# A decoder block on one core: GpSimd's convolution sums issued in halves, and one pair's weight differences moved behind the feed-forward's last split

## The chip, the cores and the metric

The kernel runs on one core of a Trainium2 chip. The metric is device microseconds from launch to the last output. It is given as the median of several runs; one more run was recorded by the hardware profiler, and all durations below come from that one.

Five engines work side by side, each through its own queue in order: PE (TensorE, matrix products, with its weight loads PEld), DVE (VectorE), ACT (ScalarE), POOL (GpSimd), and SP, which here only issues transfers. Semaphores hold an instruction back until what it needs is there.

## What is computed

The input is x, 256 tokens of width 1024, and 256 memory tokens. The reference, cut to the steps that matter here:

```
h = rms_norm(x)
u_conv, q, kc, vc, ks, vs, kw, vw, g_nsa_heads, g_conv, g_attn = split(h @ w_in)
a, gt = split(u_conv)
v = a * sigmoid(gt)
v = depthwise_causal_conv(v, conv_dw_w, width 31) + conv_dw_b
conv = silu(layer_norm(v)) @ conv_pw_w
nsa = sparse attention with 16 heads (compressed, selected, windowed keys)
x = x + (sigmoid(g_conv) * conv + sigmoid(g_attn) * nsa) @ w_out
x = x + cross_attention(rms_norm(x), mem)
a, b = split(rms_norm(x) @ ffn_in_w)
x = x + (silu(a) * b) @ ffn_out_w            # 2816 hidden units
return rms_norm(x)
```

Everything is float32.

## The kernel before

**Products.** A float32 product is made on PE from parts: each operand is split into a high part, a rounded copy, and a low part, the rest. Three products (high by high, low by high, high by low) are summed. The split of an operand is always a copy on ACT (names ending in `h`, L174 in `split`, L283 in `part`) and a subtraction on DVE that reads the operand and the copy (names ending in `l`, L175 and L284). The weights come from HBM in tiles of 128 x 1024 elements, each loaded by SP, split so, and read by PE. So PE needs a stream of ACT copies and DVE subtractions through the whole kernel.

**The convolution.** The products for `u` fill `vt` (L449), 1024 channels as eight blocks of 128 partitions, two blocks to a tile. Each block is convolved with 31 taps. The blocks are shared out. DVE makes one part in PSUM (`taps_v`, accumulator `yp`, L402 and L405), one multiply-add of 128 x 256 per tap and block. GpSimd sums the other part (`taps_g`): for each tap and pair of blocks a product tile `vw` of 128 x 512 is made, two instructions of 128 x 256, on ACT (L419) or, for every sixth tap, on GpSimd itself (L417). GpSimd then adds it to `yt` (L421). There are four buffers for `vw`, so ACT can be at most four taps ahead of GpSimd's sums. `joined` (L425) adds DVE's part to GpSimd's for the blocks that both worked on. `layer_norm_sum` (L611, L613) sums the eight blocks of `yt` into `ysum` on GpSimd, `folded` adds its two halves (L292), and PE forms the mean from it (`mu`, L619). These operations lie beside the products for `u`, `kc`, `vc`, `q`, `ks`, `kw`, `vs`, `ga` and `gc`, so that ACT and DVE carry convolution work and weight splits in one queue each.

**The feed-forward.** For each of 22 chunks j PE makes `ps_f` (L1140, L1142), then ACT and DVE make `ab` (L1143 to L1145), `sl` (L1147, L1148) and its split `uh`, `ul` (L283, L284). `marks` are the two instructions of that split of the chunk made last; after the loop they are those of chunk 21.

**The output product.** It takes 11 pairs of chunks. Six of them (`SEVEN`: 1, 2, 4, 5, 7, 8) use seven products of half-size blocks in place of eight; these need differences of weight blocks, `tr`, four DVE subtractions of 128 x 512 per pair (`side`, L1084). For pair 1, `weights_ahead` makes them early, piece by piece. For the others `weights_of_seven` loads the weights (`fo`, L1090, into the four buffers named `w`), makes `tr`, and splits weights and differences: `th`, `tl` for every other pair, `ft` for the rest. `seven_products` issues the matrix products (L1172). The tail (L1207 to L1273) adds the parts, normalizes and stores.

**The order.** A scheduler orders each engine's instructions by priority and by the times that it reckons with. `convolve` puts its instructions 1500 places behind where they are written, so that they fill gaps. `behind(*marks)` forbids that what is written inside it be issued ahead of the marks.

Of the kernel before, what the change touches and what calls it, by code (L numbers as in the profile page):

```python
# [12 lines left out]
ALU = mybir.AluOpType  # L13
# [32 lines left out]
SEVEN = (1, 2, 4, 5, 7, 8)  # L46
# [51 lines left out]
def tile_hybrid_block(  # L98
# [15 lines left out]
    nc = tc.nc  # L114
# [6 lines left out]
    def long(name, slot, shape=(P, NB, S), dt=F32):  # L121

        return sb.tile(list(shape), dt, tag=f"L{slot}", name=name)
# [9 lines left out]
    def small(name, shape, dt=F32, tag=None, bufs=1):  # L133
        return sb.tile(shape, dt, tag=tag or name, name=name, bufs=bufs)
# [31 lines left out]
    def col(base, j):  # L166
        return ppt[:, base + j:base + j + 1]


    def split(w, shape, name):  # L170
        hi = small(f"{name}h", shape, F32R, tag="whi", bufs=5)
        lo = small(f"{name}l", shape, F32R, tag="wlo", bufs=5)
        with behind(*first.get(name, ())):
            copy = nc.scalar.activation(hi, w, AF.Copy)  # L174
            splits[name] = copy, nc.vector.tensor_tensor(out=lo, in0=w, in1=f(hi[:]), op=ALU.subtract)  # L175
        return hi, lo
# [4 lines left out]
    def behind(*marks):  # L181

        stack = ExitStack()
        for m in marks:
            stack.enter_context(tc.issue_after(m.ins))
        return stack
# [22 lines left out]
    def half(src, name):  # L209
        w = small(name, list(src.shape), tag="w", bufs=4)  # L210
        nc.sync.dma_start(w, src)
        return split(w, list(src.shape), name)
# [69 lines left out]
    def part(hi, lo, src):  # L282
        copy = nc.scalar.activation(hi, src, AF.Copy)  # L283
        low = nc.vector.tensor_tensor(out=lo, in0=src, in1=f(hi), op=ALU.subtract)  # L284
        return copy, low

    def folded(a, eng):

        n = a.shape[1]
        while n > 1:  # L290
            n //= 2
            eng.tensor_tensor(out=a[:, 0:n], in0=a[:, 0:n], in1=a[:, n:2 * n], op=ALU.add)  # L292
        return a[:, 0]
# [79 lines left out]
    for i in range(4):  # L373
        hs = slice(2 * i, 2 * i + 2)
        for kb in (2 * i, 2 * i + 1):
            vec = nc.vector.scalar_tensor_tensor(out=hf[:, kb], in0=xt_t[:, kb], scalar=col(PP_GMIX, kb),
                                                 in1=r1, op0=ALU.mult, op1=ALU.mult)
# [14 lines left out]
    yt = long("yt", 6)  # L392
# [16 lines left out]
    def taps_g(j, ts):  # L409

        y = yt[:, j:j + 2]
        for t in ts:
            pr = y if t == 0 else small(f"vw{j}_{t}", [P, 2, S], tag="vw", bufs=4)
            for i in range(2):
                v, w = vt[j + i][:, t:t + S], col(PP_DW + TAPS * (j + i), t)
                if t % MIX == MIX - 1:
                    nc.gpsimd.tensor_scalar(out=pr[:, i], in0=v, scalar1=w, scalar2=0.0, op0=ALU.mult, op1=ALU.add)  # L417
                else:
                    nc.scalar.activation(pr[:, i], v, AF.Identity, scale=w, bias=col(PP_DB, j + i) if t == 0 else 0.0)  # L419
            if t > 0:  # L420
                nc.gpsimd.tensor_tensor(out=y, in0=y, in1=pr, op=ALU.add)  # L421
            yield

    def joined(j, other):
        nc.gpsimd.tensor_tensor(out=yt[:, j:j + 2], in0=yt[:, j:j + 2], in1=other, op=ALU.add)  # L425
        yield


# [1 line left out]
    taps = range(TAPS)  # L430
    on_v = chain(taps_v(0, taps[FIRST_G:], part01), taps_v(2, taps, yt[:, 2:4]), taps_v(6, taps[LAST_G:], part67))
    on_g = chain(taps_g(0, taps[:FIRST_G]), joined(0, part01), taps_g(6, taps[:LAST_G]), taps_g(4, taps), joined(6, part67))

    def convolve(n_v, n_g, *marks):
# [172 lines left out]
    ysum = small("ysum", [P, 2, S], tag="vw", bufs=4)  # L607

    def layer_norm_sum():

        nc.gpsimd.tensor_tensor(out=ysum, in0=yt[:, 0:2], in1=yt[:, 2:4], op=ALU.add)  # L611
        for j in (6, 4):
            nc.gpsimd.tensor_tensor(out=ysum, in0=ysum, in1=yt[:, j:j + 2], op=ALU.add)  # L613
        return folded(ysum, nc.gpsimd)

    def layer_norm_centre(total):
# [208 lines left out]
    nc.vector.tensor_tensor(out=sumc, in0=sumc, in1=cpt[:, CP_CM:CP_CM + 2].unsqueeze(2).to_broadcast([P, 2, HEADS]), op=ALU.mult)  # L825
    vec = nc.vector.tensor_tensor(out=nsc, in0=nsc, in1=sumc.unsqueeze(3).to_broadcast([P, 2, HEADS, 16]), op=ALU.mult)
    total = layer_norm_sum()
    rest(10)
    pct = small("pct", [P, 2, S], tag="vw", bufs=4)
    for hp, n in enumerate((7, 7, 6, 6, 6, 6, 6, 4)):  # L830
        if hp < 7:
            with behind(*[vec] * (hp == 0)):
                p.append(scores(hp + 1))
            if hp == 0:
                first["gc1_0"] = first["scores"]
                with behind(*first["scores"]):
                    hm = cpt[:, CP_HM:CP_HM + 8].unsqueeze(2).to_broadcast([P, 8, HD])
                    for i in range(2):
                        nc.vector.tensor_tensor(out=vcm[:, 8 * i:8 * i + 8], in0=vcs[:, i].unsqueeze(1).to_broadcast([P, 8, HD]),
                                                in1=hm, op=ALU.mult)  # L840
# [239 lines left out]
    def side(tr, w, n):  # L1080

        to, a, b = SIDES[n]
        pick = lambda c: tr[:, c] if isinstance(c, int) else w[c[0]][:, c[1]]
        return nc.vector.tensor_tensor(out=tr[:, to], in0=pick(a), in1=pick(b), op=ALU.subtract)  # L1084

    def weights_of_seven(i):

        w0, w1 = w = [small(f"fo{i}_{n}", [P, 2, 512], tag="w", bufs=4) for n in range(2)]
        for n in range(2):
            nc.sync.dma_start(w[n], wfo[i, n])  # L1090
        tr = long(f"tr{i}", 10, (P, 4, 512))
        for n in range(4):
            side(tr, w, n)
        b0, b1 = split(w0[:, 0:1], [P, 1, 512], f"fo{i}_0"), split(w1, [P, 2, 512], f"fo{i}_1")
        bs = [[t[:, 0] for t in b0], [t[:, 0] for t in b1], [t[:, 1] for t in b1]]
        if SEVEN.index(i) % 2 == 0:
            th, tl = (long(f"t{c}{i}", at, (P, 4, 512), F32R) for c, at in (("h", 12), ("l", 13)))
            for n in (0, 2):
                part(th[:, n:n + 2], tl[:, n:n + 2], tr[:, n:n + 2])
            ts = [[t[:, n] for t in (th, tl)] for n in range(4)]  # L1100
        else:
            ts = []
            for n in (0, 2):
                both = split(tr[:, n:n + 2], [P, 2, 512], f"ft{i}_{n}")
                ts += [[t[:, k] for t in both] for k in range(2)]
        return bs + ts
# [25 lines left out]
    for j in range(NF):  # L1132
# [16 lines left out]
        marks = part(uh[j // 8][:, j % 8], ul[j // 8][:, j % 8], sl[:])  # L1149
# [67 lines left out]
    for i in range(early):  # L1217
        if i in SEVEN:
            if i not in parts:
                parts[i] = weights_of_seven(i)  # L1220
            seven_products(i)
        else:
            for c in range(2):
                w = half(wfo[i, c], f"fo{i}_{c}")
                for tb in range(2):
                    four_products(i, c, tb, w)
# [7 lines left out]
    for i in range(early, NF // 2):  # L1234
        w = half(wfo[i, 0], f"fo{i}_0")
# [178 lines left out]
```

## Time and profile before

| | |
|---|---|
| median of 3 runs | 559.04 us (558.22 to 559.17) |
| profiled execution | 558.58 us |
| its span (first to last instruction) | 556.7 us |
| PE busy | 544.6 us, 98% |
| DVE busy | 469.2 us, 84% |
| ACT busy | 387.6 us, 70% |
| POOL busy | 147.7 us, 27% |
| granted TensorE clock | 0.999 of full speed |

The difference of 1.9 us between the profiled execution's time and its span lies around the instructions. Shares are means over the span: GpSimd's 27% is nearly all in one stretch from 46.6 to 178.6 us; most of what is left lies at 297 to 310 us and 360 to 371 us, where it sums partial squares for two norms (L923, L925, 128 x 256 each).

In the lines of a timeline, a row gives the start, the duration, the engine, the line, the operation, the tiles, and the number of instructions drawn together; brackets give the idle time ahead of it and what ended it. Rows of a line or a tile give the minimum, median and maximum of the duration in ns, then the first and the last start in us.

### The profile page before, as it was taken

What the parts mean: (1) busy time and instruction counts of PE and PEld (TensorE: products, weight loads), DVE (VectorE), ACT (ScalarE), POOL (GpSimd) and SP (SyncE); (2) the same over time, 40 slices, a digit from 0 to 9 for tenths busy, and PEclk for the clock granted to TensorE, in tenths of its full rate; (3) what the DMA queues carried; (4) which work ended last, traced back from release to release, by engine and by line L of the source; (5) the groups of instructions that cost most, each with busy time, mean ns of one, the idle gap of its engine ahead of it and who ended that gap; (6) DMA issues with size and microseconds to landing.
All of it is one profiled execution on the core that took longest, in us unless ns stands there. A gap on an engine that the chain in (4) does not pass through costs nothing. (4 is left out here: it accounts for less than half of the span.)

```text
span 556.7 us, 10584 instructions
## 1 busy us (share of the span) xinstructions
PE 544.6 (98%) x3976; PEld 505.3 (91%) x3976; DVE 469.2 (84%) x874; ACT 387.6 (70%) x724; POOL 147.7 (27%) x121
## 2 busy tenths in 40 slices
PE   9999999989999999999999999999999999999995
PEld 8999999989999998998999999988888888788884
DVE  3889998999989998895768676577899998799896
ACT  4678769999777897779646655466666676566653
POOL 0006999999998000300003100150000000000000
PEclk9999999999999999999999999999999999999999
DMA  8949725434563554335555733444646664454632
GB/s 303 400 137 323 281 92 160 155 104 166 156 225 106 170 195 131 98 109 170 189 180 177 273 118 98 172 146 159 218 153 192 200 203 161 152 174 167 195 108 75
DMA packets 29154, 97.31 MB, mean 175 GB/s; under 512 B 3120, under 2 KB 5680, under 8 KB 28848
## 3 DMA queue, kind: packets, MB, share of 16 engines
q1 hardware_dynamic: 28384, 95.42, 51.4%
q10 hardware_dynamic: 720, 1.23, 0.6%
q8 instruction: 31, 0.51, 0.4%
q14 instruction: 19, 0.16, 0.1%
HBM read 95.39 MB, written 1.25 MB: 174 GB/s over the span
## 5 line engine op out<-in xcount | busy, mean ns | idle before, releaser
L421 POOL TENSOR_TENSOR yt<-yt,vw 128x512 f32<-128x512 f32 x61 | 102.0, 1673 | 49.8 <-DVE yp L405 46.2
L419 ACT ACTIVATE vw<-vt,ppt 128x256 f32<-128x256 f32 x104 | 45.4, 498 | 8.6 <-POOL yt L421 8.3
L1140 PE MATMUL ps_f<-g,f_0h 128*128 128x512 f32 x176 | 48.4, 397 | 1.2 <-DVE ab L1144 1.2
L1140 PE MATMUL ps_f<-g,f_1h 128*128 128x512 f32 x176 | 48.9, 397 | 0.0
L405 DVE SCALAR_TENSOR_TENSOR yp<-vt,ppt,yp 128x256 f32<-128x256 f32 x108 | 45.4, 477 | 0.2
L1140 PEld LDWEIGHTS ps_f<-g,f_1h 128*128 128x128 f32 x176 | 32.8, 188 | 7.5
L1140 PEld LDWEIGHTS ps_f<-g,f_0h 128*128 128x128 f32 x176 | 30.0, 188 | 5.4 <-DVE ab L1144 1.4
L175 DVE TENSOR_TENSOR f_1l<-f,f_1h 128x1024 fp32r<-128x1024 f32 x22 | 27.5, 1248 | 4.4 <-ACT f_1h L174 2.6
L1142 PEld LDWEIGHTS ps_f<-g,f_0l 128*128 128x128 f32 x176 | 27.0, 189 | 3.9
L174 ACT ACTIVATE f_1h<-f 128x1024 fp32r<-128x1024 f32 x22 | 23.3, 1057 | 7.3 <-PE ps_xo L239 3.7
L175 DVE TENSOR_TENSOR f_0l<-f,f_0h 128x1024 fp32r<-128x1024 f32 x22 | 26.8, 1218 | 1.7 <-ACT f_0h L174 1.7
L1142 PE MATMUL ps_f<-g,f_0l 128*128 128x256 f32 x176 | 28.2, 282 | 0.0
L1142 PE MATMUL ps_f<-g,f_1l 128*128 128x256 f32 x176 | 26.5, 281 | 0.0
L174 ACT ACTIVATE f_0h<-f 128x1024 fp32r<-128x1024 f32 x22 | 23.1, 1051 | 1.3 <-PE ps_xo L239 1.3
L732 ACT ACTIVATE p<-p,mins 128x256 f32<-128x256 f32 x32 | 15.9, 502 | 10.7 <-DVE mins L717 10.7
L1142 PEld LDWEIGHTS ps_f<-g,f_1l 128*128 128x128 f32 x176 | 23.3, 188 | 0.0
L1143 ACT ACTIVATE ab<-ps_f 128x256 f32<-128x256 f32 x44 | 16.5, 376 | 8.8 <-PE ps_f L1142 8.1
L1144 DVE TENSOR_TENSOR ab<-ps_f,ab 128x256 f32<-128x256 f32 x44 | 18.3, 419 | 4.5 <-ACT ab L1143 4.2
L283 ACT ACTIVATE uh<-sl 128x256 fp32r<-128x256 f32 x22 | 9.1, 415 | 15.8 <-DVE sl L1148 15.8
L1147 ACT ACTIVATE sl<-ab 128x256 f32<-128x256 f32 x22 | 9.2, 417 | 13.6 <-DVE ab L1145 13.5
L923 POOL COPY acc<-s_wo 128x256 f32<-128x256 f32 x1 | 0.7, 658 | 63.6 <-ACT s_wo L916 63.6
L417 POOL TENSOR_SCALAR vw<-vt,ppt 128x256 f32<-128x256 f32 x18 | 16.1, 905 | 0.5
(621 smaller groups left out, 1682.9 us busy)
## 6 DMA issues: line engine op xcount, KB each, us to landing
f<-in_wst_dram SPq DMA_DIRECT2D x44, 512.0 KB, 5.4
fo<-in_wfo_dram SPq DMA_DIRECT2D x22, 512.0 KB, 3.7
u<-in_wst_dram SPq DMA_DIRECT2D x14, 512.0 KB, 6.2
q<-in_wst_dram SPq DMA_DIRECT2D x8, 512.0 KB, 5.4
ga<-in_wst_dram SPq DMA_DIRECT2D x8, 512.0 KB, 4.4
gc<-in_wst_dram SPq DMA_DIRECT2D x8, 512.0 KB, 4.6
v<-in_wst_dram SPq DMA_DIRECT2D x8, 512.0 KB, 6.5
pw<-in_wst_dram SPq DMA_DIRECT2D x8, 512.0 KB, 4.3
```

Source lines behind the costliest of these rows:

```text
L174: copy = nc.scalar.activation(hi, w, AF.Copy)
L175: splits[name] = copy, nc.vector.tensor_tensor(out=lo, in0=w, in1=f(hi[:]), op=ALU.subtract)
L405: nc.vector.scalar_tensor_tensor(out=out[:, i] if t == ts[-1] else acc[i], in0=v, scalar=w, in1=acc[i], op0=ALU.mult, op1=ALU.add)
L417: nc.gpsimd.tensor_scalar(out=pr[:, i], in0=v, scalar1=w, scalar2=0.0, op0=ALU.mult, op1=ALU.add)
L419: nc.scalar.activation(pr[:, i], v, AF.Identity, scale=w, bias=col(PP_DB, j + i) if t == 0 else 0.0)
L421: nc.gpsimd.tensor_tensor(out=y, in0=y, in1=pr, op=ALU.add)
L732: exp.append(nc.scalar.activation(p1[k][:, br], p1[k][:, br], AF.Exp, scale=-1.0, bias=mins[:, hd, 1, br:br + 1], accum_out=sums[:, hd, 1, ...
L1140: nc.tensor.matmul(ps, lhsT=hs[kb // 4][0][:, kb % 4, cs], rhs=fg[:, :, kb], start=kb == 0, stop=False)
L1142: nc.tensor.matmul(ps[:, 1], lhsT=hs[kb // 4][1][:, kb % 4, cs], rhs=fg[:, 0, kb], start=False, stop=kb == NB - 1)
L1143: nc.scalar.activation(ab[:, b], ps[:, 0], AF.Copy)
L1144: nc.vector.tensor_tensor(out=ab[:, b], in0=ps[:, 1], in1=ab[:, b], op=ALU.add)
L1147: silu = nc.scalar.activation(sl, ab[:, 0], AF.Silu)
```

## The change

Two edits are made together. The first: each of GpSimd's 66 adds of 128 x 512 in `taps_g`, `joined` and `layer_norm_sum` (61, 2 and 3 of them) is issued as two adds of 128 x 256, one for each block of the pair. The second: for pair 2, `SEVEN[1]`, the four differences `tr2` are issued behind `marks`, the split of chunk 21.

```
-            if t > 0:
-                nc.gpsimd.tensor_tensor(out=y, in0=y, in1=pr, op=ALU.add)
+            for i in range(2 if t else 0):
+                nc.gpsimd.tensor_tensor(out=y[:, i], in0=y[:, i], in1=pr[:, i], op=ALU.add)
...
     def joined(j, other):
-        nc.gpsimd.tensor_tensor(out=yt[:, j:j + 2], in0=yt[:, j:j + 2], in1=other, op=ALU.add)
+        for i in range(2):
+            nc.gpsimd.tensor_tensor(out=yt[:, j + i], in0=yt[:, j + i], in1=other[:, i], op=ALU.add)
...
-        nc.gpsimd.tensor_tensor(out=ysum, in0=yt[:, 0:2], in1=yt[:, 2:4], op=ALU.add)
-        for j in (6, 4):
-            nc.gpsimd.tensor_tensor(out=ysum, in0=ysum, in1=yt[:, j:j + 2], op=ALU.add)
+        for i in range(2):
+            nc.gpsimd.tensor_tensor(out=ysum[:, i], in0=yt[:, i], in1=yt[:, 2 + i], op=ALU.add)
+        for j in (6, 7, 4, 5):
+            nc.gpsimd.tensor_tensor(out=ysum[:, j % 2], in0=ysum[:, j % 2], in1=yt[:, j], op=ALU.add)
...
         tr = long(f"tr{i}", 10, (P, 4, 512))
-        for n in range(4):
-            side(tr, w, n)
+        with behind(*marks if i == SEVEN[1] else ()):
+            for n in range(4):
+                side(tr, w, n)
```

The lines below the edits move down: L425 becomes L426, L611 and L613 become L613 and L615, L1084 becomes L1086, L1144 becomes L1147.

On GpSimd, in the middle of the convolution, before (names with the pair of blocks and the tap, `vw0_14`, and a buffer number):

```order
L421 TENSOR_TENSOR yt_359<-yt_359,vw0_14_832 128x512
L417 TENSOR_SCALAR vw0_17_918<-vt0_351,ppt_66 128x256 x2
L421 TENSOR_TENSOR yt_359<-yt_359,vw0_15_836 128x512
L421 TENSOR_TENSOR yt_359<-yt_359,vw0_16_914 128x512
L421 TENSOR_TENSOR yt_359<-yt_359,vw0_17_918 128x512
```

And the same place after:

```order
L421 TENSOR_TENSOR yt_359<-yt_359,vw0_14_845 128x256 x2
L421 TENSOR_TENSOR yt_359<-yt_359,vw0_15_850 128x256
L417 TENSOR_SCALAR vw0_17_934<-vt0_351,ppt_66 128x256 x2
L421 TENSOR_TENSOR yt_359<-yt_359,vw0_15_850 128x256
L421 TENSOR_TENSOR yt_359<-yt_359,vw0_16_929 128x256 x2
L421 TENSOR_TENSOR yt_359<-yt_359,vw0_17_934 128x256 x2
```

Each row of 128 x 512 has become two of 128 x 256 with the same inputs in the same order; now and then another instruction slips between the two.

On DVE, in the last chunks of the feed-forward, before (`tr2` the differences of pair 2, `fo2` its weights, `ab19` and `ab20` the results of chunks 19 and 20):

```order
L1148 TENSOR_TENSOR sl18_5972<-sl18_5972,ab18_5932 128x256
L1074 TENSOR_TENSOR sr8_5913<-sl17_5908,sr8_5913 128x128
L1084 TENSOR_TENSOR tr2_6226<-fo2_0_6222 128x512
L284 TENSOR_TENSOR ul2_4804<-sl18_5972,uh2_4801 128x256
L284 TENSOR_TENSOR bl1_1_5978<-fo1_5121,bh1_1_5977 128x512
L1144 TENSOR_TENSOR ab19_5993<-ps_f19_0_5994,ab19_5993 128x256
L1144 TENSOR_TENSOR ab20_6054<-ps_f20_0_6055,ab20_6054 128x256
L175 TENSOR_TENSOR f21_1l_6108<-f21_1_6105,f21_1h_6107 128x1024
```

The same place on DVE after:

```order
L1151 TENSOR_TENSOR sl18_6038<-sl18_6038,ab18_5998 128x256
L1076 TENSOR_TENSOR sr8_5979<-sl17_5974,sr8_5979 128x128
L284 TENSOR_TENSOR ul2_4870<-sl18_6038,uh2_4867 128x256
L284 TENSOR_TENSOR bl1_1_6044<-fo1_5187,bh1_1_6043 128x512
L1147 TENSOR_TENSOR ab19_6059<-ps_f19_0_6060,ab19_6059 128x256
L1147 TENSOR_TENSOR ab20_6120<-ps_f20_0_6121,ab20_6120 128x256
L175 TENSOR_TENSOR f21_1l_6174<-f21_1_6171,f21_1h_6173 128x1024
```

The first difference of pair 2 no longer stands ahead of the `ab` of chunks 19 and 20; the others stood further down, among the rows of chunks 20 and 21, and are gone from there too.

Further down on DVE, after, at the end of chunk 21 (`ft2` are the splits of the differences):

```order
L1151 TENSOR_TENSOR sl21_6217<-sl21_6217,ab21_6177 128x256
L284 TENSOR_TENSOR ul2_4870<-sl21_6217,uh2_4867 128x256
L1086 TENSOR_TENSOR tr2_6292<-fo2_0_6288 128x512
L1086 TENSOR_TENSOR tr2_6292<-fo2_1_6289,fo2_0_6288 128x512
L1086 TENSOR_TENSOR tr2_6292<-fo2_1_6289,tr2_6292 128x512 x2
L175 TENSOR_TENSOR ft2_0l_6306<-tr2_6292,ft2_0h_6305 128x1024
L175 TENSOR_TENSOR ft2_2l_6310<-tr2_6292,ft2_2h_6309 128x1024
```

All four now stand in one block right behind the split of chunk 21, with the two splits made from them next.

## Prediction

> **What bounds the kernel now.** I read the page's first part, then busy time in three stretches of the convolution, then the waits of PE.
>
> ```profile
> PE 544.6 (98%) x3976; PEld 505.3 (91%) x3976; DVE 469.2 (84%) x874; ACT 387.6 (70%) x724; POOL 147.7 (27%) x121
> ```
>
> ```profile
> 46.00:179.00 133.00, 129.34 (x1097) 126.09 (x1096) 126.92 (x215) 111.70 (x221) 127.60 (x85) 1.00 0.52 173
> 84.00:98.00 14.00, 14.00 (x117) 13.68 (x117) 12.40 (x27) 13.82 (x26) 13.47 (x11) 1.00 0.57 150
> 112.00:126.00 14.00, 11.61 (x97) 11.24 (x96) 13.71 (x23) 13.79 (x30) 13.51 (x12) 1.00 0.36 116
> ```
>
> (Columns: stretch, length, busy time of PE, PEld, DVE, ACT, POOL.) Over the span PE is the bound. In the convolution's 133 us four engines are: GpSimd has work for 127.60 of them, DVE for 126.92, and ACT for 13.8 of 14 us in the middle stretches. GpSimd's 27% hides that.
>
> ```profile
> PE vc_ps L538 <- DVE zz L527: 1.3, 1, 1.3
> PE ps_f L1140 <- DVE ab L1144: 1.2, 1, 1.2
> PE kc_ps L533 <- DVE zz L525: 1.1, 1, 1.1
> PE cb_ps L469 <- DVE vt L449: 0.8, 1, 0.8
> PE s L712 <- DVE nsc L676: 0.4, 1, 0.4
> ```
>
> PE waits 3.6 us in the convolution (1.3 + 1.1 + 0.8 + 0.4), always for DVE, and 1.2 us once in the feed-forward. So little can be won: 4.8 us at most, and only 1.2 of it at the second edit's place. Much can be lost if GpSimd, with 127.60 of 133 us taken, gets slower.
>
> **The first edit: the price of a half.** GpSimd's adds of the convolution, those of the other norms, and rows of the timeline:
>
> ```profile
> L421 POOL TENSOR_TENSOR yt<-yt,vw x61: 1268/1308/2292, 46.6 to 173.9; 128x512 f32<-128x512 f32 x61
> L925 POOL TENSOR_TENSOR acc<-acc,s_wo x7: 797/805/922, 297.2 to 309.2; 128x256 f32<-128x256 f32 x7
> L925 POOL TENSOR_TENSOR acc<-acc,s_xo x7: 747/913/1622, 360.7 to 370.5; 128x256 f32<-128x256 f32 x7
> ```
>
> ```profile
> 171.25 1.30 POOL L613 TENSOR_TENSOR ysum<-ysum,yt 128x512 f32<-128x512 f32 x1
> 172.50 2.68 POOL L421 TENSOR_TENSOR yt<-yt,vw 128x512 f32<-128x512 f32 x2
> ```
>
> An undisturbed add of 512 takes 1.30 us. One of 256, the same operation on the same type, takes 0.80, not 0.65. Of two adds in a row, the second starts 1.25 us behind the first (171.25, 172.50), so 0.05 overlaps. A pair of halves then takes 0.80 + 0.75 = 1.55 us where one took 1.30: 0.25 more. With 66 such adds that is 16.5 us more work for GpSimd. The lower end is a half at half the price: nothing added. The upper end is two halves at the median of the `s_xo` row, 0.913, with the same overlap: 1.78, or 0.48 more, 31.7 us. The shortest row of a half, 0.747, against the shortest of a whole, 1.268, gives 0.18 more, 11.6 us; two halves of 0.80 with no overlap give 0.30, 19.8 us. I take 0.25, which lies between the near rows.
>
> The Trainium skill, GPSIMD Engine Reference, section "3.1 Elementwise — side-by-side cycle accounting", measures an add of 2048 elements per partition at 4497 ns, in proportion to the elements. By it 512 elements are 1.12 us, which would leave 0.18 of the measured 1.30 as a fixed share (an estimate from that page and the row); the sum by it would end near 560.
>
> **From GpSimd to PE.** GpSimd's own end is not the issue: its sums end at 178.64 and PE reads them much later.
>
> ```profile
> 176.96 1.69 POOL L292 TENSOR_TENSOR ysum<-ysum 128x256 f32<-128x256 f32 x1
> L619 PE MATMUL mu<-ysum,ones x2: 378/378/378, 204.5 to 204.7; 128*128 128x256 f32 x2
> ```
>
> That leaves 25.9 us. The path is ACT's queue. ACT makes the tap products and the high parts of the weights in one order, and can be only four tap tiles ahead of GpSimd:
>
> ```profile
> ACT vw L419 <- POOL yt L421: 8.3, 6, 2.7
> L174 ACT ACTIVATE ks_0h<-ks x1: 1050/1050/1050, 110.2 to 110.2; 128x1024 fp32r<-128x1024 f32 x1
> L239 PEld LDWEIGHTS ps_ks<-hh,ks_0h x8: 187/188/191, 120.7 to 121.5; 128*128 128x128 f32 x8
> L174 ACT ACTIVATE vs_0h<-vs x1: 1052/1052/1052, 123.9 to 123.9; 128x1024 fp32r<-128x1024 f32 x1
> L239 PEld LDWEIGHTS ps_vs<-vs_0h,hh x8: 187/188/189, 134.0 to 134.8; 128*128 128x128 f32 x8
> ```
>
> ACT already stands 8.3 us for GpSimd, so it is at the buffers' limit in places, and a GpSimd that falls behind takes ACT along. ACT's lead over PE is 9.4 us for `ks_0h` (110.2 + 1.05 to 120.7) and 9.0 for `vs_0h` (123.9 + 1.05 to 134.0). I take 9 us: GpSimd's first 9 us of delay are hidden by it. Of 16.5 us spread evenly over the 132 us from 46.6, 9 are used up after 72 us, near 119; every later tap tile then holds back a weight copy that PE is ready for. PE loses 16.5 - 9 = 7.5 us. If the cover were absent, all 16.5 would show; with 0.14 more per pair or less, none.
>
> **What DVE gets back.** A DVE subtraction reading two SBUF tiles and a GpSimd add hold each other up:
>
> ```profile
> 46.00:179.00 133.00, 59.91 (x37) 1.00 0.52 173
> 200.00:360.00 160.00, 49.65 (x41) 1.00 0.49 160
> ```
>
> These are the L175 subtractions in the convolution and behind it: 1.62 us each against 1.21, so 37 x 0.41 = 15 us of DVE's time go into waiting for GpSimd. A half holds for about half as long, so DVE may get back 7.5 us. What PE can gain from this is bounded by its waits: 0 to 3.6 us. Two thirds of these are for `zz`, a short chain behind PE's own product, which shorter weight subtractions don't cut. I take 0.5 us.
>
> **The second edit.** DVE, PE and the transfers around the first difference of pair 2:
>
> ```profile
> 483.38 0.69 DVE L1084 TENSOR_TENSOR tr<-fo 128x512 f32<-128x512 f32 x1 [3.19 <-DMA fo<-in_wfo_dram]
> 483.99 0.42 DVE L284 TENSOR_TENSOR ul<-sl,uh 128x256 fp32r<-128x256 f32 x1
> 484.32 0.68 DVE L284 TENSOR_TENSOR bl<-fo,bh 128x512 fp32r<-128x512 f32 x1
> 484.93 0.75 DVE L1144 TENSOR_TENSOR ab<-ps_f,ab 128x256 f32<-128x256 f32 x2
> ```
>
> ```profile
> 485.40 1.20 PE L1140 MATMUL ps_f<-g,f_0h 128*128 128x512 f32 x4 [1.22 <-DVE ab L1144]
> ```
>
> DVE stands 3.19 us for the transfer of `fo2`, with `ab` of chunks 19 and 20 queued behind it, and PE stands 1.22 us for that `ab`. With the difference behind chunk 21's split, nothing waits for the transfer there: the 1.22 us go.
>
> What it costs is later work on pair 2. The four differences (0.61 apart by the starts 483.38 and 483.99, 2.4 together) now start when chunk 21 is split:
>
> ```profile
> 497.41 0.63 PE L1142 MATMUL ps_f<-g,f_1l 128*128 128x256 f32 x4
> 505.10 0.40 PE L1172 MATMUL m<-ft_0h,sh 128*128 128x512 f32 x1
> 506.26 0.40 PE L1172 MATMUL m<-ft_0l,sh 128*128 128x512 f32 x1
> 503.16 0.68 DVE L1084 TENSOR_TENSOR tr<-fo 128x512 f32<-128x512 f32 x1
> ```
>
> Chunk 21's product ends at 498.0, then 496.8 less the stall; `ab`, `sl` and the split take about 2.6 us (five DVE operations of 0.4 to 0.7 and two of ACT), so 499.4. Two differences and ACT's copy of 1.05 us make `ft2_0h` ready at 501.7, against a use at 505.10 - 1.2 = 503.9; `ft2_0l` is ready at 503.0 against 505.1. Some 2 us are left. SP's queue is moved too: pair 4's load takes the buffer that pair 2's `fo2_0` frees, and its issue goes from 491.6 us,
>
> ```profile
> 491.61 7.66 SPq L1090 DMA_DIRECT2D fo<-in_wfo_dram x2
> fo<-in_wfo_dram SPq DMA_DIRECT2D x22, 512.0 KB, 3.7
> ```
>
> to about 500.6; landing 3.7 us later, 504.3, it is 1.1 us late for its first difference (503.16 before). At the end DVE, not PE, closes the kernel, with little idle time among its last sums:
>
> ```profile
> 544.17 0.69 DVE L1207 TENSOR_TENSOR y<-fo,more 128x512 f32<-128x512 f32 x1 [0.38 <-PE fo L1172]
> 547.90 0.69 DVE L1259 TENSOR_TENSOR y<-fo,more 128x512 f32<-128x512 f32 x1 [0.52 <-PE fo L1172]
> ```
>
> So of PE's 1.2 us at most 0.9 (0.38 + 0.52) can pass through DVE's queue there unless that queue too runs earlier. Ends: -1.2 us, and +3 if the late loads reach PE. I take -0.6.
>
> **The sum.** 558.58 + 7.5 - 0.5 - 0.6 = 565.0 us. The profiled execution is 0.46 us under the median shown, less than the difference that I call none: 0.2%, 1.1 us, which is about what a measurement of this kernel can tell.
>
> **The rivals.**
>
> Faster, because halves let DVE in sooner. For it: DVE is nearly full in the convolution, loses 15 us to GpSimd there, and every wait of PE is for DVE, none for ACT or GpSimd. Against it: a half at 0.80. It decides at 0.14 us more per pair, a pair at 1.44: up to there ACT's 9 us hide GpSimd's delay and DVE's gain is all that PE sees. The time is 558.58 - 0.6 less 0 to 3.6, so 554.4 to 558, likeliest 556.5. The Trainium skill, SBUF — State Buffer, section "🔬 SBUF: two separate sides", calls the shared port pair an exclusive lock, held for a whole instruction while the other engine is fully blocked. By that rule the wait halves with the instruction; the trace agrees that they block (1.62 us against 1.21). I give this 0.20.
>
> No change: both sides cancel, with 0.16 more per pair (10.6 - 9 = 1.6 lost, 1.1 won): 559.1. Only a narrow band of prices gives this: 0.08.
>
> A larger loss: the price near its upper end (0.48 x 66 = 31.7, less 9, so 580), or no lead of ACT at the small stages around `vt`, `zz` and `nsc`, where PE had already waited (558.58 + 16.5 - 1.1 = 574). For it: those waits stand in the rows, with no slack. Against it: the `s_xo` median may hold other waits, and ACT's lead is there for every weight I looked at. 0.09.
>
> The forecast, and on top of it a loss at the end: the 1.1 us by which pair 4's transfer is late, or more, reaches PE, which then stands 1 to 3 us in the output product: 566 to 568. Against it: the 2 us left above. 0.08.
>
> **How the numbers follow.** The forecast has 0.55, with a price of 0.18 to 0.30 and so 560 to 570 us by itself; its middle is 565. Slower is 0.55 + 0.09 + 0.08 = 0.72, faster 0.20, same 0.08. The range goes from 556 to 573: below it lies a part of the faster case, 0.06, above it most of the larger loss, 0.08.
>
> **What would show each step.** Half adds at 0.80 us and a convolution stretch on GpSimd that ends near 190 us or later instead of 178.6; ACT waiting for GpSimd far longer than 8.3 us; new waits of PE for ACT copies from about 119 us on; L175 subtractions nearer 1.4 than 1.62 us in the convolution; and no 1.22 us wait of `ps_f` for `ab`. I am wrong if a half follows its twin at 0.70 us or less, if GpSimd's stretch gets no longer because its own waits for DVE shrink too, or if ACT's lead grows as fast as it is used up.

## The result and the profile after

The changed kernel takes 565.86 us (median of 4 runs, 565.78 to 566.51), the kernel before 559.11 in the same comparison (558.22 to 559.25). The ratio is 1.0127, interval 1.0109 to 1.0144: slower by 6.8 us, under 2% but clear of the noise. The forecast was 565.0 in 556 to 573. The profiled execution took 565.78 us with a span of 563.6, 6.9 more than before.

First the page of the changed kernel, then the waits of PE:

```profile
PE 545.3 (97%) x3976; PEld 505.6 (90%) x3976; DVE 473.8 (84%) x874; ACT 388.8 (69%) x724; POOL 157.4 (28%) x187
```

```profile
PE kc_ps L534 <- DVE zz L526: 7.8, 1, 7.8
PE cb_ps L470 <- DVE vt L450: 2.2, 1, 2.2
PE s L714 <- DVE nsc L678: 0.4, 1, 0.4
```

PE works 0.7 us longer than before (545.3 against 544.6), and is idle 18.3 us against 12.1 (span less busy). Two waits have grown: for `zz` from 1.1 to 7.8, for `vt` from 0.8 to 2.2. Two are gone: `vc_ps` for `zz` (1.3) and `ps_f` for `ab` (1.2). That makes 5.6 of the 6.2 us.

In the stretch of the long wait the granted clock is low as well (same columns as in the prediction):

```profile
98.00:112.00 14.00, 14.00 (x142) 13.34 (x141) 14.00 (x11) 12.02 (x26) 13.04 (x19) 1.00 0.16 55
112.00:126.00 14.00, 6.99 (x60) 6.79 (x58) 13.85 (x25) 12.33 (x26) 13.13 (x15) 0.92 0.45 149
126.00:140.00 14.00, 13.17 (x97) 13.17 (x98) 13.65 (x25) 12.63 (x25) 14.00 (x16) 0.84 0.51 165
```

DVE is busy throughout, but from 98 to 112 with 11 instructions, where it did 24 before. The timelines of DVE and of GpSimd at that place:

```profile
98.56 9.30 DVE L175 TENSOR_TENSOR q_1l<-q,q_1h 128x1024 fp32r<-128x1024 f32 x1
107.78 0.87 DVE L405 SCALAR_TENSOR_TENSOR yp<-vt,ppt,yp 128x256 f32<-128x256 f32 x2
```

```profile
98.41 8.37 POOL L421 TENSOR_TENSOR yt<-yt,vw 128x256 f32<-128x256 f32 x12
107.74 4.51 POOL L421 TENSOR_TENSOR yt<-yt,vw 128x256 f32<-128x256 f32 x5 [0.96 <-ACT vw L419]
```

One weight subtraction, 1.21 us where GpSimd is idle, stands from 98.56 to 107.86. In that time GpSimd makes 12 half adds, 0.70 us apart, with no gap. The subtraction ends 1.08 us after the twelfth add, in the pause in which GpSimd waits for ACT. Everything in DVE's queue is then about 8 us late, `zz` among it, at 126.5 instead of 118.6.

The halves of `taps_g`, and behind them the busy time and number of DVE's L175 subtractions in the convolution:

```profile
L421 POOL TENSOR_TENSOR yt<-yt,vw x122: 714/740/1808, 44.8 to 183.1; 128x256 f32<-128x256 f32 x122
```

```profile
46.00:179.00 133.00, 60.82 (x36) 0.97 0.52 172
```

A half takes 0.74 us, and the next starts 0.70 us after it. Without the long one, 35 subtractions take 51.5 us, 1.47 each in place of 1.62.

At the second edit's place, DVE after (chunk 21's split and the four differences), and among the last sums:

```profile
507.83 0.43 DVE L284 TENSOR_TENSOR ul<-sl,uh 128x256 fp32r<-128x256 f32 x1 [1.40 <-ACT uh L283]
508.18 0.68 DVE L1086 TENSOR_TENSOR tr<-fo 128x512 f32<-128x512 f32 x1
```

```profile
551.22 0.68 DVE L1210 TENSOR_TENSOR y<-fo,more 128x512 f32<-128x512 f32 x1
554.87 0.68 DVE L1262 TENSOR_TENSOR y<-fo,more 128x512 f32<-128x512 f32 x1
```

The two `y` rows have no idle time ahead of them, where the kernel before had 0.38 and 0.52: DVE's queue is now full there. The same matmuls start 7.06 us later than before up to chunk 20, 5.57 later behind the place of the old `ab` wait, 6.42 later at the last products, and the last operations of DVE 6.96 later. So the edit wins 1.49 us and gives back 0.85 in the output product and 0.54 in the tail.

### The profile page after: what moved, and what is told of

It reads as the page before. It is cut to its first block, busy times and chain, and to the rows that moved or that the text cites. A ratio compares the mean times of both kernels' runs of the same rounds, so it can differ in the third digit from the quotient of the medians.

```text
span 563.6 us, 10698 instructions
## 1 busy us (share of the span) xinstructions
PE 545.3 (97%) x3976; PEld 505.6 (90%) x3976; DVE 473.8 (84%) x874; ACT 388.8 (69%) x724; POOL 157.4 (28%) x187
## 4 chain that ended last, share of the span: by engine, by line
PE 65%; DVE 18%; issue 8%; DMA 3%; POOL 2%; ACT 2%; ACTq 0%; DVEq 0%; SPq 0%; POOLq 0%
PE ps_f L1143 15%; PE ps_f L1145 7%; DVE yp L405 6%; PE ps_pw L239 4%; PE ps_xq L239 4%; PE ps_wo L239 4%; PE ps_xo L239 4%; PE ps_v L239 4%; PE ps_gc L239 4%; PE ps_k L239 3%; PE ps_u L239 3%; DMA fo<-in_wfo_dram 2%; PE ps_ga L239 2%; POOL yt L421 2%; DVE fo_1l L175 2%
## 5 line engine op out<-in xcount | busy, mean ns | idle before, releaser
L421 POOL TENSOR_TENSOR yt<-yt,vw 128x256 f32<-128x256 f32 x122 | 115.7, 983 | 47.8 <-ACT vw L419 46.7
L175 DVE TENSOR_TENSOR f_1l<-f,f_1h 128x1024 fp32r<-128x1024 f32 x22 | 27.5, 1248 | 5.9 <-ACT f_1h L174 4.0
L175 DVE TENSOR_TENSOR f_0l<-f,f_0h 128x1024 fp32r<-128x1024 f32 x22 | 26.8, 1218 | 1.7 <-ACT f_0h L174 1.7
L1146 ACT ACTIVATE ab<-ps_f 128x256 f32<-128x256 f32 x44 | 16.5, 375 | 10.6 <-PE ps_f L1145 9.8
L1147 DVE TENSOR_TENSOR ab<-ps_f,ab 128x256 f32<-128x256 f32 x44 | 18.3, 419 | 5.0 <-ACT ab L1146 4.7
L174 ACT ACTIVATE fo_1h<-fo 128x1024 fp32r<-128x1024 f32 x10 | 10.6, 1056 | 7.8 <-DMA fo<-in_wfo_dram 4.7
```

What stands on the lines that cost most here:

```text
L421: nc.gpsimd.tensor_tensor(out=y[:, i], in0=y[:, i], in1=pr[:, i], op=ALU.add)
L1146: nc.scalar.activation(ab[:, b], ps[:, 0], AF.Copy)
L1147: nc.vector.tensor_tensor(out=ab[:, b], in0=ps[:, 1], in1=ab[:, b], op=ALU.add)
```

## The experiments

GpSimd's time can be taken apart for each profile: its own work without disturbance (instructions and the short gaps or overlaps between them), what DVE's subtractions added to single instructions, and long gaps, in which it waits. The stretch goes from its first to its last operation of the convolution. PE's idle and busy time are those of the whole span. The medians given below the table are over all runs of a kernel; a ratio need not be the quotient of two of them.

| kernel | stretch | own work | held by DVE | long gaps | PE idle | PE busy | ratio to before |
|---|---|---|---|---|---|---|---|
| two_acc | 131.0 | 93.7 | 33.0 | 4.4 | 11.3 | 544.9 | 1.0014 (0.9991 to 1.0038) |
| before | 132.0 | 99.0 | 33.0 | 0 | 12.1 | 544.6 | 1 |
| tr_only | 132.3 | 98.9 | 33.4 | 0 | 12.9 | 544.8 | 1.0016 (1.0004 to 1.0029) |
| halves_mix | 133.5 | 93.4 | 34.8 | 5.2 | 12.4 | 543.7 | 0.9968 (0.9956 to 0.9980) |
| extra | 138.4 | 103.9 | 34.0 | 0.5 | 14.5 | 549.7 | 1.0120 (1.0077 to 1.0164) |
| halves5 | 139.5 | 101.5 | 36.7 | 1.3 | 13.4 | 548.7 | 1.0111 (1.0051 to 1.0172) |
| zigzag | 139.7 | 101.5 | 36.8 | 1.3 | 14.0 | 548.3 | 1.0112 (1.0095 to 1.0129) |
| halves_only | 139.8 | 101.5 | 36.8 | 1.5 | 16.8 | 548.7 | 1.0116 (1.0095 to 1.0137) |
| run_whole | 141.0 | 101.9 | 35.0 | 4.1 | 15.8 | 546.9 | 1.0107 (1.0086 to 1.0129) |
| the change | 141.5 | 101.7 | 35.9 | 3.9 | 18.3 | 545.3 | 1.0127 (1.0109 to 1.0144) |
| zigzag_forced | 143.8 | 107.0 | 35.1 | 1.7 | 18.0 | 548.6 | 1.0153 (1.0111 to 1.0194) |

The loss has two parts in this table. PE idles longer, and in most of the kernels that lost it is also busy longer with the same products: 3.7 to 5.1 us in extra, halves5, zigzag, halves_only and zigzag_forced, 2.3 in run_whole, 0.7 in the change. The granted clock goes with it. Its mean over the span is 0.983 to 0.991 in every run of the seven kernels that lost, and 0.990 to 0.999 in the runs of the other four. One stretch in three kernels, before, zigzag and halves_only (columns as above):

```profile
168.00:182.00 14.00, 14.00 (x114) 13.63 (x114) 13.79 (x40) 9.27 (x24) 10.41 (x7) 1.00 0.29 97
168.00:182.00 14.00, 13.00 (x87) 12.84 (x88) 11.04 (x31) 9.95 (x26) 14.00 (x17) 0.77 0.45 147
168.00:182.00 14.00, 11.42 (x64) 11.27 (x65) 13.78 (x34) 7.39 (x23) 14.00 (x15) 0.62 0.59 196
```

In 13.00 and 11.42 us of busy time PE makes 87 and 64 products there, where it made 114 in 14.00 before. (The kernels that lost are some us further back in their sequence, so these are not the very same products.)

**Which edit: the two apart.** Only the first edit (halves_only), and only the second (tr_only).

```
halves_only: the first three hunks of the change; tr_only: the last one
```

> Only the first edit: GpSimd's 66 adds in halves; the differences of pair 2 stay where they were. Theory A (DVE is shut out): halves that don't depend on each other follow without a gap, GpSimd keeps the port, one weight subtraction of DVE stands about 9 us, and PE waits about 8 us for zz: 565.5 to 567 us, with a single L175 subtraction of 8 us or more and a PE wait for zz of 7 us or more, as in the changed kernel. Theory B (the price of a half, as predicted: GpSimd is slower, ACT falls behind, PE waits): 564 to 567 us too, but with the loss spread over several waits and no single long subtraction. Theory C (the second edit makes the loss): 559 us.

It took 564.95 us against 558.78. Its interval overlaps that of the change, so the first edit alone gives the loss, as far as these runs can tell. The waits of PE and one row of DVE's timeline:

```profile
PE s L714 <- DVE nsc L678: 3.2, 1, 3.2
PE ps_ga L239 <- ACT sga L649: 2.6, 1, 2.6
PE cb_ps L470 <- DVE vt L450: 1.7, 1, 1.7
```

```profile
162.28 4.94 DVE L175 TENSOR_TENSOR ga_1l<-ga,ga_1h 128x1024 fp32r<-128x1024 f32 x1 [2.75 <-ACT ga_1h L174]
```

The loss is the same, the places are others: PE waits for `zz` only 0.5 us, and stands twice between 162 and 171 us instead, once for ACT and once for DVE. The longest stand of a subtraction is 4.94 us here. So neither theory is met in full: the loss is spread, as B said, but there is a long stand.

> Only the second edit: pair 2's four differences behind the split of chunk 21, GpSimd's adds whole. Predicted: PE's wait of 1.22 us for ab goes, 0.6 us come back as profit: 558.4 us. Rival: the output product and the tail give all of it back (later weights, DVE's last sums): 559.0, within 0.3 of the kernel before. If the second edit makes the loss of the change: 565.

559.99 us against 558.78, 0.16% slower with an interval from 0.04 to 0.29%. The wait for `ab` is gone, and PE, 1.19 us behind the kernel before at that time, is 0.30 ahead of it after; the tail ends 1.02 behind. So 1.3 of the 1.5 us are given back there. The 1.2 us by which it was behind came before 205 us, in waits of 0.2 to 0.5 us, far from the place of the edit. No gain, and less than the 0.6 us forecast.

**Is it DVE that is shut out?** Two kernels meant to let DVE in sooner.

```
zigzag:     for i in ((0, 1) if t % 2 else (1, 0)) if t else ():
                (add of half i)
run_whole:  if t > 0 and not (j == 0 and 15 <= t <= 22): (two halves)
            elif t > 0: (one whole add)
```

> Halves as in the first edit, but each tap adds its two halves in the other order than the tap before (0 1, 1 0, 0 1 ...), so that every second add reads what the add just ahead of it wrote and must wait for it. Work and instruction count are those of halves_only. Theory A: these waits reopen the port at least every 1.5 us; no L175 subtraction stands more than 2.5 us, PE's wait for zz falls to 2 us or less, 559 to 561 us. Theory B: GpSimd gets slower still by the waits (66 x 0.08 = 5 us): 566 to 570 us.

565.17 us against 558.78. The scheduler put the halves back into an order without waits (0.70 us apart, no gap of 0.08 between them), so this is the same first edit in a second profile. It is useful as such: no subtraction stands over 1.9 us here, and the loss is the same. Being shut out for long is therefore not needed for the loss. What this profile has instead is ACT behind GpSimd:

```profile
ACT vw L419 <- POOL yt L421: 15.7, 18, 2.9
```

and PE's waits:

```profile
PE ps_ga L239 <- ACT sga L649: 2.6, 1, 2.6
PE cb_ps L470 <- DVE vt L450: 1.8, 1, 1.8
PE s L714 <- DVE nsc L678: 1.8, 1, 1.8
```

ACT stands 15.7 us for GpSimd, 8.3 before. Its `sga`, which frees the bank that PE needs, comes 4.3 us later than before (165.40 against 161.09).

> Halves everywhere except in the taps 15 to 22 of the first pair of blocks, where the adds are whole as before (8 of 66). That is where the subtraction stood 9.3 us. Theory A: the long stand goes if no other run of halves takes its place: 559 to 561.5 us, and no subtraction over 3 us. Theory B: 58 of 66 adds are still halves, so 58/66 of the loss stays: 564.5 to 566 us.

564.43 us against 558.78. The forecast misplaced the stand: it lies in the taps 3 to 8 of blocks 6 and 7, which GpSimd sums after the first pair, not in the taps made whole. A stand of 8.65 us at 99.22 came back there. So this run says only that eight whole adds elsewhere change nothing that can be measured.

**Is it GpSimd's pace?** Theory P says that the time follows from how long GpSimd takes, whatever the form of its adds. Four runs: halves made to wait, no halves but more work, whole adds without waits, and one more buffer.

```
zigzag_forced:  as zigzag, each half inside "with behind(previous half)"
extra:          if t % MIX == 2:
                    nc.gpsimd.tensor_scalar(out=idle, in0=pr, scalar1=2.0, ...)
two_acc:        to = yo if t % 2 else y        # whole adds, joined at the last tap
                nc.gpsimd.tensor_tensor(out=to, in0=to, in1=pr, op=ALU.add)
halves5:        tag="vw", bufs=5
```

> Halves in alternating order (0 1, 1 0, 0 1 ...), and the order fixed: each half is issued behind the half before it. So every second half add reads what the add just ahead of it wrote, and waits for it. No work is added. In the kernel before such a wait leaves 0.08 us between two adds, where independent halves overlap by 0.04, so GpSimd needs about 0.12 x 60 = 7 us more than halves_only. Theory P (pace: what counts is how long GpSimd takes, which holds back ACT through the four buffers): 569 to 574 us. Theory A (DVE is shut out by adds without a gap, the pace is not what counts): no subtraction of DVE over 2.5 us, 558 to 562 us.

568.26 us against 558.96. No subtraction stands long, the stretch is 4 us longer than in halves_only, and the median is higher still. The interval overlaps that of halves_only, so the sign is P's without being certain; the size is 0.7 us under its range.

> The kernel before, adds whole, with 11 more GpSimd instructions in the convolution: a product of 128 x 512 into a tile that nobody reads, one per six taps. At about 0.85 us each, with some blocked by DVE, they take GpSimd 9 to 13 us. Nothing is halved. Theory P: the same loss as the change, 564 to 570 us, with waits of PE for vt, zz, nsc or the gates and the TensorE clock lowered behind them. Theory A: 558.5 to 560.5 us, since ACT's lead hides it.

566.28 us against 558.96: the same loss with whole adds. The added products took 0.64 us (median) instead of 0.85, and the stretch grew by 6.4. PE is idle 2.4 us more than before and busy 5.1 us more. Its waits:

```profile
PE cb_ps L471 <- ACT rel_sb L475: 4.3, 1, 4.3
PE cs_ps L675 <- DVE part L405: 1.3, 1, 1.3
```

One reservation: the added product also reads the `vw` tile and so holds its buffer, and ACT waited 7.1 us for it, next to 9.9 for the sums.

> Adds whole, but in two sums: even taps in yt, odd taps in a second tile, joined by one add at the end of each pair of blocks (the number of adds stays the same). No add reads what the one ahead of it wrote, so the 0.08 us between adds go and GpSimd saves 0.12 x 50 = 6 us. Theory P: GpSimd's stretch gets about 6 us shorter, PE's waits in the convolution shrink: 556.5 to 558.5 us. Theory A: adds without a gap shut out DVE here too: a subtraction of over 4 us, 561 to 568 us.

560.18 us against 558.96, not told apart from it, and in neither theory's range. GpSimd's own work fell by 5.3 us as expected, but the stretch only by 1.0: it then waited 4.4 us itself. No subtraction stood over 2.4 us, though the adds had no gaps.

> Halves as in halves_only, with five buffers for the products in place of four. Theory P by way of the buffers: ACT may be one tap further ahead, 2.1 us of lead, so one to three of the 6 us come back: 561.5 to 564 us. If the buffers aren't the way by which GpSimd's pace reaches PE: 564.5 to 566 us.

564.31 us against 558.96. Within the error of halves_only, and just above the 561.5 to 564 us that P expected by way of the buffers: a fifth buffer changes nothing that can be measured. ACT still stands 14.3 us for GpSimd's sums.

**Take work from GpSimd.** If pace is the cause, halves must cost nothing once GpSimd has less to do.

```
halves_mix:  MIX = 40                       # ACT makes all products
halves_f20:  FIRST_G, LAST_G = 20, 9        # four taps to DVE, and in convolve's calls
             convolve((14, 13, 10, 2)[j], (5, 4, 4, 3)[j], act, vec)
whole_f20:   the same with whole adds
two_f21:     two_acc with FIRST_G, LAST_G = 21, 10
```

> Halves as in halves_only, but GpSimd makes no products: the 18 of 128 x 256 that it made for every sixth tap are made on ACT. GpSimd loses 15 us of work, ACT gets 18 x 0.45 = 8 us more. Theory P: GpSimd's stretch falls from 139.8 us to about 125, under the 132 of the kernel before, and the loss goes: 557.5 to 560 us. Rival (halves cost by themselves, whatever GpSimd's total): 563.5 to 566 us. Rival (ACT, which has under 0.5 us idle of 14 in the middle, is overloaded): 561 to 564 us, with waits of PE for ACT.

557.25 us against 559.24, ratio 0.9968 (0.9956 to 0.9980): faster than the kernel before, with every add in halves. GpSimd's stretch is 133.5 us, 6.3 less than in halves_only (not 125: its own work fell by 8.1 us, not 15, and it then waits 5.2 us), and the granted clock stays at 1.00:

```profile
46.00:179.00 133.00, 130.93 (x1119) 128.49 (x1118) 126.23 (x221) 120.62 (x241) 127.40 (x132) 1.00 0.54 177
```

PE's longest wait in the convolution:

```profile
PE cb_ps L470 <- ACT rel_sb L474: 2.1, 1, 2.1
```

> Halves as in halves_only, and four taps moved from GpSimd and ACT to DVE (three of the first pair of blocks, one of the third): GpSimd loses four sums, about 7.5 us, DVE gets 16 products of 0.43, less the 8 it would have had... in all 8 more, 3.4 us, which is what shorter waits for GpSimd gave it back (59.9 to 52 to 56 us for its L175 subtractions). Theory P: GpSimd's stretch about 132 us as before: 557.5 to 560 us. Rival (halves cost by themselves): 563 to 566 us.

> The kernel before, adds whole, with the same four taps moved to DVE. GpSimd's stretch falls to about 125 us; DVE has 3.4 us more and gets nothing back. Theory P, if GpSimd's pace still bounds the kernel before: 556.5 to 558.5 us. If DVE is the tighter one there: 559 to 562 us.

> Two sums with whole adds, as in two_acc, and two taps of the first pair of blocks moved to DVE: GpSimd 3.5 us less, DVE 1.7 us more. Theory P with DVE as the next bound: no gain over two_acc, 558 to 560 us. If GpSimd's pace still bounds it: 557 us.

572.43, 571.81 and 565.66 us against 559.24: ratios 1.0239 (1.0224 to 1.0254), 1.0217 (1.0197 to 1.0238) and 1.0119 (1.0099 to 1.0139). All three missed by far, with whole adds as with halves. The waits of PE in halves_f20:

```profile
PE cs_ps L675 <- DVE part L405: 10.0, 1, 10.0
PE cb_ps L470 <- ACT rel_sb L474: 3.4, 1, 3.4
```

`cs_ps` is written into a bank of the tag that DVE's accumulators `yp` use, so PE waits there for the end of DVE's convolution: 10.0 us here, 9.0 in whole_f20, 5.0 in two_f21. DVE's taps have an end of their own on PE's path, and moving taps to DVE (and their calls, in the first two) pushes it back. GpSimd's stretch in whole_f20 was 129.0 us, 3 us shorter than before, and the kernel lost all the same. So GpSimd's pace is not the only way to such a loss; these three have another one, say nothing on the pace, and are not in the table.

## Why the prediction was right, and where it was not

The direction was right for a reason that held, slower sums on GpSimd. The number (565.0 against 565.86) is luck: the price was too high, the cover too large, and the clock was not in the sum. By my own list of signs, a half that follows its twin at 0.70 us or less would show me wrong; it follows at 0.70.

*The price of a half.* Forecast 0.80 us, and 0.25 us more for a pair. Measured: 0.74 us, 0.70 apart, so a pair takes 1.40 where a whole add with its gap took 1.37. Undisturbed, the halves cost GpSimd 2.7 us in all (101.7 against 99.0), not 16.5. The rows of the prediction were of other norms' sums, and why those adds take longer is not shown; the shortest of them, 0.747, was the right one. What I left out is the gap: the whole adds, each of which read the sum before, had 0.08 us between them, while halves overlap by 0.04, and this pays for most of their fixed cost. The stretch still grew by 9.5 us: 2.7 of own work, 2.9 held by DVE, 3.9 of waits of its own. For the second, a subtraction that holds up a half costs GpSimd 0.94 us (35.9 over 38 instructions), a whole add 0.87 (33.0 over 38).

*The cover.* I let ACT's lead of 9 us hide the first 9 us of delay. With the measured 0.14 us per pair (9.5 / 66) my own rule gave no loss. It was wrong: in the table, stretches 6.4 to 11.8 us longer than before cost 6.0 to 8.6 us. Not all of that is lack of cover, since PE's idle time grew by 1.3 to 6.2 us alone and the rest is its longer busy time. The lead that I measured was that of weight copies, and no wait of PE for one shows in the changed kernel. PE waits at `vt`, `zz`, `sga` and `nsc`, small stages without that lead. I had them among the rivals, "no lead of ACT at the small stages", at 0.09.

*The path.* That GpSimd's slower pace would reach PE by ACT's queue is borne out for halves_only and zigzag, where ACT stands 12.8 and 15.7 us for GpSimd. In the profile of the change it stands 8.0, not more than before; there the way leads over DVE and its subtraction of 9.30 us. That GpSimd's pace is the common cause is shown from two sides, by extra (loss without halves) and halves_mix (halves without loss). Each has a reservation: the added products of extra also hold `vw` buffers, and halves_mix gives ACT more to do. A rival is the order, since each variant is scheduled anew. The traces speak against it for the change, halves_only and zigzag: up to 205 us PE's order is that of before, DVE's differs by the place of one instruction and ACT's by the places of eight from 135 to 162 us, and as many of ACT's instructions (228) stand ahead of the first `sga` as before. Why one profile takes the one way and another the other is open.

*What DVE gets back.* Forecast up to 7.5 us in its subtractions. Measured in the stretch from 46 to 179 us: 3.6 in halves_only and, with one subtraction fewer in the window, 7.7 in zigzag (56.30 and 52.24 against 59.91). It didn't show while GpSimd was behind. With GpSimd relieved the kernel came to 557.25, in the "faster" rival's range of 554.4 to 558. That fits the rival's mechanism, decided by GpSimd's total and not by the price of a half alone, but does not show it: whether whole adds would gain as much with ACT's products is not known.

*The clock.* It wasn't in the sum. In zigzag PE is idle only 1.9 us more than before and yet busy 3.7 us more. Four stretches of its profile behind the wait of 1.84 us for `vt`, which ended at 83.92:

```profile
84.50:85.50 1.00, 1.00 (x11) 1.00 (x11) 1.00 (x4) 0.66 (x2) 1.00 (x3) 1.00 0.61 201
85.50:86.00 0.50, 0.50 (x5) 0.50 (x5) 0.50 (x3) 0.50 (x2) 0.50 (x1) 0.65 1.04 344
86.00:88.50 2.50, 2.50 (x13) 2.50 (x13) 0.73 (x2) 2.40 (x6) 2.50 (x5) 0.50 0.50 105
89.00:90.00 1.00, 1.00 (x10) 1.00 (x10) 1.00 (x3) 0.99 (x3) 1.00 (x2) 0.97 0.23 35
```

The clock falls to half for about 3.4 us, and PE loses 1.48 us more (the same matmuls start 1.55 us late ahead of it, 3.03 behind). The rest of the 3.7 us belongs to a second fall, that of the row from 168 to 182 us above, again behind waits of PE. What sets off a fall is open. At the first place one also followed a wait of 1.17 us in halves5 and of 1.97 in run_whole, and none followed 1.74 in halves_only and 2.25 in the change; the kernel before had waits up to 1.3 us and no fall. So a wait of PE can cost more than its own length, and these runs don't say which one will.

*The second edit.* The wait went as forecast (1.22 us in the row, 1.49 by the starts). The profit of 0.6 didn't come: 1.39 was given back (0.85 + 0.54). Chunk 21's split ended at 508.26, 4.7 us behind its product, where the working gave 2.6: DVE stood for ACT's `uh` (1.40 us in the row above). That took the 2 us or so that I had counted as spare for `ft2`. Where in the output product PE loses the 0.85 stays open, since the list of waits names none there. The 0.54 in the tail is what the prediction had named, DVE's queue without idle time.

## What to carry to other kernels

An engine that is nearly idle over the span can set the pace of a stretch: look at each stretch, and at who is held back by its buffers. When a lead is to hide a delay, look for the steps on the path with the least of it, not the typical one. Count a wait of PE together with what its clock does behind it: idle time alone was less than half of the loss in three of the kernels here. Before an instruction is split, ask what the whole one waited for: the split may take a dependency away, and with it a gap that pays for part of its price.

## What had not been expected of the hardware

A DVE subtraction of two SBUF tiles, 1.21 us where GpSimd is idle, took 9.30 us beside 12 half adds 0.70 us apart, and 8.65 and 4.94 us in two other kernels. It ended 1.08 us after the row of adds, which reads as GpSimd shutting it out. The Trainium skill, SBUF — State Buffer, section "🔬 SBUF: two separate sides", says that the loser waits for the other's instruction; here it waited, by that reading, for a row of them. Most subtractions among such halves were let in after the first (1.2 to 1.75 us), and two_acc, with adds that overlap as well, shows no such stand, so what decides is open.
